# A one-core decoder block: the MLP's first product by seven quadrant products, a second product of its own stage, one DRAM record per retention chunk

## The chip, the core and the metric

The kernel runs on one core of a Trainium2 chip. A core has a matrix engine (TensorE, PE in the profile, its weight loads PEld), three engines for elementwise work (VectorE = DVE, ScalarE = ACT, GpSimd = POOL), and SyncE (SP), whose queue issues nearly all DMAs of this kernel. Each engine takes its instructions in one fixed order and waits for the others through semaphores. The metric is the device time of one execution in microseconds (us). The time of the kernel before is 2742.19 us, the median of 3 runs (2741.0 to 2742.73).

## The reference, cut to what matters

One layer on 1024 tokens of width 1024, float32:

```
h = rms_norm(x, g_mix);  z = h @ w_in                    # 1024 x 13312
rq, rk, rv, rg, dq, dk, dv, cq, gates = split_cols(z)
ret  = swish(rg) * head_norm(retention_chunkwise(rq, rk, rv))   # 4 heads, chunks of 128
y_ret, y_diff, y_cross = ret @ w_ret_o, da @ w_diff_o, ca @ w_cross_o
merged = g0 * y_ret + g1 * y_diff + g2 * y_cross
x = x + merged @ w_out
u = relu(rms_norm(x, g_ffn) @ w_up);  x = x + (u * u) @ w_down    # width 4096
out = rms_norm(x, g_final)
```

`rms_norm(x, g)` multiplies every token by its own factor 1/sqrt(mean(x*x) + eps) and every feature by g.

## The kernel before, in words

**Layout and arithmetic.** Activations are kept feature-major: 128 features in the partitions, 512 tokens (half of the sequence, t = 0 or 1) along a row. Every float32 operand is split into a high part (a CAST on ACT, L141) and a low part (a subtraction on DVE, L142) by `split`, and every product is three matmuls, high by high, high by low, low by high (`mm3`, L154 to L156).

**Stages.** In order of time in the profile: the start and the norm (to 90 us), the combined input projection (to 1128), cross-attention (to 1200), differential attention (to 1437), retention (to 1816), the rest of the retention branch's output projection (to 1930), `w_out` and the second norm (to about 2021), the MLP (to 2732), and the last norm.

**The seven-product scheme** (`left_operands` L207, `quad` L226, `seven` L240) serves the input projection in both kernels. A unit is 256 output columns by all 1024 tokens over all 1024 features. Cut into quadrants it would take eight products of 4 x 3 matmuls of 128x512; Strassen's scheme in Winograd's form takes seven, from four sums of weight quadrants (`add` on DVE in `left_operands`) and four sums of activation quadrants (made once, called T1 to T4), with B11, B21, B22 the plain quadrants. Results are combined through copies s1 to s3 and additions in `emit`. The projection has 52 units.

**Scratch in DRAM.** The projection's results go to DRAM and are read back by the branches. For retention these are several tensors: `zh_d` (q and k, split, 512 tokens of a head), `zt_d` (k and v transposed, split) and `z_d` (the swish gate). For chunk c of head h, `ret_prepare` (L806) computes the masked 128x128 scores (`rsc`) and loads v (two DMAs, L821) and transposed k (L827); `ret_inputs` (L797) loads q and k of a whole head in four DMAs; `ret_product` (L830) makes the chunk's output (`ro`) and the new state (`rst`, `Sf`, `Shl`); `ret_store` (L890), one chunk later, transposes the output (`rot`), loads the gate (`sg`, two DMAs, L898), multiplies on DVE (`spill`) and stores to `rn_d` (two DMAs, L901).

**Fill.** `branch_halves` (L488) is a generator; each step is one product `y` of 24 matmuls of 128x512 of a branch's output projection, multiplied by its gate `g` (loaded, L495) and added to the running sum `m`, which is loaded from and stored to DRAM (`mg_d`, L498, L505). `fill` takes such steps between the chunks of attention and retention; the lists `FILL_D` and `FILL_R` say how many. In differential attention 16 steps of the cross branch run, in retention 16 of the differential branch and about half of the 32 of the retention branch; `drain` takes the rest. `ad_load` (L791) and `ret_features` (L906) read the branches' results back from DRAM, 256 KB a DMA, and split them; they use the `hf` buffers, of which there are two.

**MLP.** `mlp_up` (L1003) makes one 128-wide slice f of u for each token half by 24 matmuls (`fm_gemm`), then relu, square, split; `mlp_down` (L1018) multiplies two slices at a time by `w_down` and adds the 16 results `dn` into `x2` in SBUF on DVE (L1032). The two alternate, so u never leaves SBUF. PSUM has 8 banks: 3 `mm`, 3 `at`, 2 `sc`.

**Order.** Instructions are traced in the program's order, which gives their priority; the framework then fixes each engine's order when the kernel is compiled, and may take a later instruction that is ready by its own reckoning ahead of an earlier one that is not. A pool's memory that another pool used waits tile by tile for its release.

## Time and profile before

| | us |
|---|---|
| median of 3 runs | 2742.19 (2741.0 to 2742.73) |
| the profiled execution's own time | 2745.52 |
| its span, first to last instruction | 2743.7 |
| PE busy in it | 2624.5 (96%) |
| DVE busy | 1550.9 (57%) |
| ACT busy | 979.0 (36%) |

The page has the busy time of each engine, the span in 40 slices, the DMA queues, the chain that ended last, the costliest groups of instructions and the DMA issues. A matmul's time in a row overlaps its neighbours': a 128x512 one shows about 390 ns, and they follow each other faster than that. What one costs is read from how many fit into a stretch in which PE never rests.

### The profile page before, as it was taken

The page shows a single profiled execution, that of the slowest core. Times are in us where ns is not written, and L with a number is a line of the kernel's source. Part 1 is how long each engine was busy: PE and PEld are TensorE (multiplying, and loading weights), DVE is VectorE, ACT ScalarE, POOL GpSimd, SP SyncE. Part 2 cuts the span into 40 slices and gives each one's busy share as a digit, 9 for nine tenths or more (in the row PEclk, how much of TensorE's full clock was granted, in tenths as well). Part 3 has the DMA queues.
Part 4 walks back from the last instruction along what each step waited for, and adds up shares of the span by engine and source line. Part 5 has one row for each costly group of instructions (what it writes and reads, how often), then busy time and mean ns, then how long its engine had stood idle before and what let it go on. Part 6 is the DMA issues. An engine that isn't in the chain of part 4 may idle for free.

```text
span 2743.7 us, 32286 instructions
## 1 busy us (share of the span) xinstructions
PE 2624.5 (96%) x12070; PEld 2139.7 (78%) x12070; DVE 1550.9 (57%) x2745; ACT 979.0 (36%) x1784; POOL 84.9 (3%) x103
## 2 busy tenths in 40 slices
PE   7899999999999999799987898899999999999998
PEld 6688887887888888688875676768788888888887
DVE  6756556665566544377665556544664454544445
ACT  4444444444444444355553223221431212121222
POOL 3000000000000000001110000000000000000001
PEclk9999999999999999999998999989999999999999
DMA  5444447645533332545538878855421111111111
GB/s 204 166 162 170 161 143 222 207 154 149 155 104 111 112 104 92 199 171 194 193 122 292 273 255 257 261 175 166 142 85 46 47 46 54 43 58 47 46 39 62
DMA packets 250221, 390.40 MB, mean 142 GB/s; under 512 B 16720, under 2 KB 150864, under 8 KB 243920
## 3 DMA queue, kind: packets, MB, share of 16 engines
q1 hardware_dynamic: 249920, 388.30, 43.1%
q8 instruction: 95, 1.56, 0.2%
q14 instruction: 62, 0.51, 0.1%
q10 hardware_dynamic: 144, 0.03, 0.0%
HBM read 260.35 MB, written 127.93 MB: 142 GB/s over the span
## 4 chain that ended last, share of the span: by engine, by line
PE 56%; issue 27%; DMA 8%; DVE 6%; ACT 2%; SPq 1%; POOL 1%; POOLq 0%; DVEq 0%; ACTq 0%
PE x L154 12%; PE x L156 12%; PE x L155 12%; PE y L154 3%; PE y L156 3%; PE y L155 3%; DMA g<-z 2%; DMA adr<-da 2%; DMA arr<-rn 1%; PE wo L155 1%; PE wo L156 1%; PE zt L449 1%; PE wo L154 1%; DVE hop L142 1%; DVE g L159 1%
## 5 line engine op out<-in xcount | busy, mean ns | idle before, releaser
L154 PE MATMUL x<-hop,wo 128*128 128x512 f32 x1456 | 572.4, 393 | 6.1 <-ACT wo L141 5.4
L155 PE MATMUL x<-hop,wo 128*128 128x512 f32 x1456 | 574.0, 394 | 0.0
L156 PE MATMUL x<-hop,wo 128*128 128x512 f32 x1456 | 571.5, 393 | 0.0
L154 PEld LDWEIGHTS x<-hop,wo 128*128 128x128 f32 x1456 | 274.1, 188 | 64.6 <-ACT wo L141 5.8
L156 PEld LDWEIGHTS x<-hop,wo 128*128 128x128 f32 x1456 | 274.1, 188 | 58.9 <-DVE wo L142 0.2
L155 PEld LDWEIGHTS x<-hop,wo 128*128 128x128 f32 x1456 | 273.9, 188 | 58.6
L141 ACT CAST whl<-wst 128x1024 fp32r<-128x1024 f32 x112 | 115.9, 1048 | 398.4 <-PE dn L156 257.2
L1032 DVE TENSOR_TENSOR x<-x,dn 128x512 f32<-128x512 f32 (+1 forms) x248 | 164.5, 669 | 128.0 <-PE dn L156 127.6
L155 PE MATMUL dn<-u,whl 128*128 128x512 f32 (+1 forms) x544 | 207.3, 381 | 0.0
L154 PE MATMUL dn<-u,whl 128*128 128x512 f32 (+1 forms) x544 | 206.4, 379 | 0.0
L156 PE MATMUL dn<-u,whl 128*128 128x512 f32 (+1 forms) x544 | 204.5, 376 | 0.0
L155 PE MATMUL u<-h,whl 128*128 128x512 f32 x512 | 200.5, 392 | 0.0
L154 PE MATMUL u<-h,whl 128*128 128x512 f32 x512 | 200.0, 391 | 0.0
L141 ACT CAST wo<-wr 128x512 fp32r<-128x512 f32 x208 | 129.0, 622 | 198.9 <-PE x L156 193.3
L156 PE MATMUL u<-h,whl 128*128 128x512 f32 x512 | 199.4, 389 | 0.0
L159 DVE TENSOR_TENSOR zo<-x,s 128x512 f32<-128x512 f32 x156 | 107.6, 690 | 156.0 <-ACT s L269 106.2
L142 DVE TENSOR_TENSOR wo<-ws,wo 128x512 fp32r<-128x512 f32 x156 | 107.7, 691 | 154.8 <-ACT wo L141 154.8
L142 DVE TENSOR_TENSOR wo<-wr,wo 128x512 fp32r<-128x512 f32 x208 | 142.8, 688 | 69.8 <-ACT wo L141 61.2
L1010 DVE TENSOR_TENSOR ur<-ur 128x512 f32<-128x512 f32 x64 | 44.3, 692 | 194.9 <-ACT ur L1009 194.9
L142 DVE TENSOR_TENSOR whl<-wst,whl 128x1024 fp32r<-128x1024 f32 x112 | 135.4, 1220 | 26.7 <-ACT whl L141 26.6
L1009 ACT ACTIVATE ur<-u 128x512 f32<-128x512 f32 x64 | 38.2, 598 | 233.4 <-PE u L156 233.4
L159 DVE TENSOR_TENSOR g<-y,g 128x512 f32<-128x512 f32 x64 | 44.2, 690 | 133.3 <-PE y L156 80.3
(227 smaller groups left out, 4664.0 us busy)
## 6 DMA issues: line engine op xcount, KB each, us to landing
wr<-in_w_z SPq DMA_DIRECT2D x104, 512.0 KB, 3.8
zh<-zh SPq DMA_DIRECT2D x80, 512.0 KB, 3.5
zt<-zth SPq DMA_DIRECT2D x64, 512.0 KB, 3.8
z<-zo SPq DMA_DIRECT2D x80, 256.0 KB, 2.0
g<-z SPq DMA_DIRECT2D x64, 256.0 KB, 4.6
vhl<-zt SPq DMA_DIRECT2D x64, 256.0 KB, 4.6
wst<-in_w_up SPq DMA_DIRECT2D x32, 512.0 KB, 3.3
wst<-in_w_down SPq DMA_DIRECT2D x32, 512.0 KB, 3.3
```

Of the source, the lines that this page charges most:

```text
L141: nc.scalar.copy(out=hl_hi, in_=src)
L142: eng.tensor_tensor(out=hl_lo, in0=src, in1=hl_hi.bitcast(F32), op=ALU.subtract)
L154: nc.tensor.matmul(out, ah, bh, start=first, stop=False, skip_group_check=again)
L155: nc.tensor.matmul(out, ah, bl, start=False, stop=False, skip_group_check=again)
L156: nc.tensor.matmul(out, al, bh, start=False, stop=last, skip_group_check=again)
L159: nc.vector.tensor_tensor(out=out, in0=a, in1=b, op=op)
L449: nc.tensor.transpose(out=tp[:, i * P : (i + 1) * P], in_=st[:, i * P : (i + 1) * P], identity=ident)
L1009: nc.scalar.activation(out=r, in_=o, func=AF.Relu)
L1010: nc.vector.tensor_tensor(out=r, in0=r, in1=r, op=ALU.mult)
L1032: nc.vector.tensor_tensor(out=x2[d][t][:, cols], in0=x2[d][t][:, cols], in1=o[:, :width], op=ALU.add)
```

## The change

The first product of the MLP is computed by the seven-product scheme, in 16 units, on activations that carry the feature factor `g_ffn` but not the token factor; that factor multiplies the results in `u_emit` before the square (relu commutes with a positive factor). The results go to DRAM (`u_d`), x after the mixer goes there too (`xs_d`), and the second product is a stage of its own that reads both back, with four slices in a product instead of two. In retention, q, k, v, transposed k and the gate of one chunk lie side by side in one DRAM record (`rc_d`, 12 KB a partition), loaded by one DMA; the projection's stores into it become runs of 128 tokens (512 bytes). The running sum of the branches stays in SBUF from the differential branch on (`x2`). Results are read back in pairs (`pair_load`). Four fill steps of the cross branch move from differential attention to the first two retention chunks. PSUM becomes 2 `mm`, 3 `at`, 3 `sc`.

```diff
-FILL_D = [[1, 0] * 4] * 4
-FILL_R = [[1] * 8] * 4
+FILL_D = [[1, 0] * 4] * 2 + [[1, 0, 0, 0] * 2] * 2
+FILL_R = [[2, 2] + [1] * 6] + [[1] * 8] * 3
+C_K, C_Q, C_V, C_KT, C_G, C_N = 0, 512, 1024, 2048, 2560, 3072
...
-        return ps.tile([P, HALF], F32, tag="mm", name=name, bufs=3)
+        return ps.tile([P, HALF], F32, tag="mm", name=name, bufs=2)
...
-        return ps.tile([P, HALF], F32, tag="sc", name=name, bufs=2)
+        return ps.tile([P, HALF], F32, tag="sc", name=name, bufs=3)
...
+        def store_chunks(h, base, width, at, tile):
+            for a in range(2):
+                o = base + a * width + at
+                nc.sync.dma_start(
+                    out=rc_d[h][t][:, :, o : o + P], in_=tile[:, a].rearrange("p (i c) -> p i c", i=4).bitcast(F32)
+                )
...
+                if mode == 1:
+                    nc.sync.dma_start(out=x2[d][t], in_=mg_d[d][t])
                 add(g, o, g, ALU.mult)
+                if mode == 0:
+                    nc.sync.dma_start(out=mg_d[d][t], in_=g)
                 else:
+                    add(x2[d][t], x2[d][t], g)
...
+    def pair_load(src, outs):
+        raw = rawp.tile([P, 4, 2, P], F32, tag="pr", name="pr", bufs=2)
+        nc.sync.dma_start(out=raw, in_=src)
+        for e, o in enumerate(outs):
+            by = o.rearrange("p a (i c) -> p a i c", i=4)
+            split(by[:, 0], by[:, 1], raw[:, :, e])
...
+    def ret_prepare(h, c):
+        rec = rp.tile([P, C_N], F32R, tag="rec", name="rec", bufs=3)
+        nc.sync.dma_start(out=rec.bitcast(F32), in_=rc_d[h][c // 4][:, c % 4])
...
+            if h == 0 and c == 2:
+                drain()
+                ad_load()
+                halves = branch_halves(1, w_do, 0, hl_rhs(ad), 1)
...
+                add(xr, o, xr)
+                nc.sync.dma_start(out=xs_d[d][t], in_=xr)
+                nc.scalar.activation(
+                    out=x3[kp][t][:, a], in_=xr, func=AF.Copy, scale=vec[:, V_FFN + d : V_FFN + d + 1]
+                )
+                sq = zs_tile("acc", "acc") if acc is None else zs_tile("sq", "sq", 1)
+                nc.scalar.activation(out=sq, in_=xr, func=AF.Square)
...
+                    nc.gpsimd.tensor_tensor(out=acc, in0=acc, in1=sq, op=ALU.add)
+            if t == 1:
+                for a in range(2):
+                    operand(h2p, hop2, kp, (B11, B21)[a], x3[kp][0][:, a])
+                operand(h2p, hop2, kp, B22, x3[kp][1][:, 1])
+                t1 = h2p.tile([P, HALF], F32, tag="tt", name="t1", bufs=4)
+                add(t1, x3[kp][1][:, 0], x3[kp][0][:, 0], ALU.subtract)
+                add(x3[kp][0][:, 0], x3[kp][1][:, 1], t1, ALU.subtract)
+                t1s.append(t1)
...
+    def u_emit(u, n, t, a, b):
+        st = zs_tile("sp", "uo", 3)
+        if b is not None:
+            add(st, a, b)
+            a = st
+        nc.vector.scalar_tensor_tensor(out=st, in0=a, scalar=0.0, in1=rows[t], op0=ALU.max, op1=ALU.mult)
+        nc.scalar.activation(out=st, in_=st, func=AF.Square)
+        nc.sync.dma_start(out=u_d[2 * u + n][t], in_=st)
+    for key, t in ((T3, 1), (T4, 0)):
+        for kp in range(4):
+            df = h2p.tile([P, HALF], F32, tag="tt", name="df", bufs=4)
+            nc.gpsimd.tensor_tensor(out=df, in0=x3[kp][t][:, 1], in1=x3[kp][t][:, 0], op=ALU.subtract)
+            operand(h2p, hop2, kp, key, df)
+    seven(list(range(16)), hop2, lambda u: left_operands(wu, w_up[u, 0], w_up[u, 1]), ut, u_emit)
...
+    FC = 4
+    CHUNKS = [range(0, 2), range(2, 4)] + [range(f, f + FC) for f in range(4, 32, FC)]
+    x2 = [[dw.tile([P, HALF], F32, name=f"xm{d}_{t}", tag=f"xm{d}_{t}", bufs=1) for t in range(2)] for d in range(8)]
...
-    mlp_up(range(3))
-    for c in range(nchunk - 2):
-        mlp_up([3] if c == 0 else range((c + 1) * FC, (c + 2) * FC))
+    nxt = down_chunk(0)
+    for d in range(8):
         for t in range(2):
+            nc.sync.dma_start(out=x2[d][t], in_=xs_d[d][t])
+    for c in range(len(CHUNKS)):
+        cur = nxt
+        if c + 1 < len(CHUNKS):
+            nxt = down_chunk(c + 1)
+            for t in range(2):
+                mlp_down(cur, t)
```

## Rows read from the trace of the kernel before

**Rows 1.** The page's busy time of each engine, and its 40 slices of PE
```profile
PE 2624.5 (96%) x12070; PEld 2139.7 (78%) x12070; DVE 1550.9 (57%) x2745; ACT 979.0 (36%) x1784; POOL 84.9 (3%) x103
...
PE   7899999999999999799987898899999999999998
```

**Rows 2.** Busy time by stretch: from:to, us, engines, clock, DMA share, GB/s
```profile
450.00:480.00 30.00, 28.33 (x135) 22.28 (x133) 19.49 (x31) 14.38 (x26) 0.00 (x0) 1.00 0.69 214
...
1127.00:1147.00 20.00, 7.54 (x38) 6.78 (x38) 6.86 (x13) 7.83 (x16) 0.00 (x0) 0.70 0.86 319
...
1200.00:1437.00 237.00, 228.24 (x1316) 191.00 (x1314) 162.55 (x522) 126.77 (x343) 25.11 (x32) 1.00 0.45 155
...
1437.00:1455.00 18.00, 4.62 (x17) 3.99 (x18) 1.17 (x4) 1.75 (x6) 0.39 (x1) 0.56 1.00 371
...
1455.00:1816.00 361.00, 324.69 (x1469) 257.40 (x1468) 217.85 (x470) 101.56 (x165) 19.21 (x32) 0.96 0.80 255
...
1816.00:1930.00 114.00, 108.03 (x425) 81.62 (x423) 44.27 (x60) 22.00 (x31) 0.00 (x0) 0.91 0.51 166
...
2070.00:2670.00 600.00, 600.00 (x2630) 493.43 (x2629) 282.05 (x381) 115.69 (x164) 0.00 (x0) 1.00 0.15 47
```

**Rows 3.** Groups by shape: the MLP's matmuls, and the elementwise work that moves
```profile
L155 PE MATMUL u<-h,whl 128*128 128x512 f32 x512 | 200.5, 392 | 0.0
...
L155 PE MATMUL dn<-u,whl 128*128 128x512 f32 x480 | 188.9, 394 | 0.0
...
L142 DVE TENSOR_TENSOR wo<-wr,wo 128x512 fp32r<-128x512 f32 x208 | 142.8, 688 | 69.8 <-ACT wo L141 61.2 <-DMA wr<-in_w_z 8.7
...
L141 ACT CAST wo<-wr 128x512 fp32r<-128x512 f32 x208 | 129.0, 622 | 198.9 <-PE x L156 193.3 <-DMA wr<-in_w_z 4.3 <-issue 1.3
...
L358 POOL TENSOR_TENSOR xr<-xr 128x512 f32<-128x512 f32 x4 | 6.5, 1634 | 6.2 <-DVE tt L159 6.2
```

**Rows 4.** Timeline of the projection's end and the next stage's first matmul
```profile
1127.96 0.40 PE L156 MATMUL x<-hop,wo 128*128 128x512 f32 x1
...
1132.16 0.85 SPq L541 DMA_DIRECT2D cq<-zh  x2
...
1138.94 0.55 PE L154 MATMUL csc<-mk,cq 128*128 128x256 f32 x1 [10.58 <-DMA cq<-zh]
```

**Rows 5.** Timeline of the start, where POOL and DVE work side by side
```profile
74.92 1.65 POOL L358 TENSOR_TENSOR xr<-xr 128x512 f32<-128x512 f32 x1 [2.43 <-DVE tt L159]
75.37 1.75 DVE L159 TENSOR_TENSOR tt<-xr,tt 128x512 f32<-128x512 f32 x1
```

**Rows 6.** The chain that ended last, at the start of retention
```profile
1436.61 7.54 DMA rk<-zh
...
1444.63 10.99 DMA adr<-da
```

**Rows 7.** Timeline of retention chunks: scores, transposes, the gate's multiplication
```profile
1710.33 0.22 PE L154 MATMUL rsc<-rq,rk 128*128 128x128 f32 x1
...
1710.39 0.27 PE L155 MATMUL rsc<-rq,rk 128*128 128x128 f32 x1
...
1714.61 0.60 PE L893 MATMUL rot<-ident,on 128*128 128x128 f32 x4
...
1812.26 0.60 PE L893 MATMUL rot<-ident,on 128*128 128x128 f32 x4
...
1813.48 0.67 DVE L159 TENSOR_TENSOR spill<-rot,sg 128x512 f32<-128x512 f32 x1
```

**Rows 8.** DMA issues: count, KB each, median us from issue to landing
```profile
zh<-zh SPq DMA_DIRECT2D x80, 512.0 KB, 3.5
zt<-zth SPq DMA_DIRECT2D x64, 512.0 KB, 3.8
...
cq<-zh SPq DMA_DIRECT2D x8, 1024.0 KB, 4.9
...
rk<-zh SPq DMA_DIRECT2D x8, 1024.0 KB, 7.5
```

More of the change, by code (lines that the diff above doesn't have):

```diff
@@ L26 @@
 NH = 4
-NA, NRAW, NLOW = 27, 3, 6
 LAM_INIT = 0.8 - 0.6 * math.exp(0.0)
@@ L110, in hybrid_block @@
     nc.vector.memset(mhalf, -0.5)
-    def pairs(name, n):
-        return [[dram.tile([P, 2, HALF], F32, name=f"{name}{i}_{t}", tag=f"{name}{i}_{t}") for t in range(2)] for i in range(n)]
     def scratch(name, shape):
@@ L486, in fm_gemm, with branch_halves @@
         return out
-    def branch_halves(b, w, w0, rhs, before, out=None):
+    def branch_halves(b, w, w0, rhs, mode):
         for d in range(8):
@@ new lines, in hybrid_block @@
+        rows.append(acc)
+    for kp in range(4):
+        operand(h2p, hop2, kp, T2, x3[kp][0][:, 0])
+    for kp in range(4):
+        operand(h2p, hop2, kp, T1, t1s[kp])
+    for t in range(2):
+        rb = rms_finish(rows[t], HALF)
+        rows[t] = zs_tile("hf", "row")
+        nc.scalar.copy(out=rows[t], in_=rb)
+    wpx.close()
+    ux = ExitStack()
+    wu = ux.enter_context(tc.tile_pool(name="wu", bufs=2, side="right", reuse_waits="tile"))
+    ut = ux.enter_context(tc.tile_pool(name="ut", bufs=2, side="right", reuse_waits="tile"))
@@ new lines, in down_chunk @@
+    def down_chunk(c):
+        ws, us = [], [[], []]
+        for f in CHUNKS[c]:
+            for t in range(2):
+                raw = dw.tile([P, HALF], F32, tag="ur", name="ur", bufs=4)
+                nc.sync.dma_start(out=raw, in_=u_d[f][t])
+                u = dw.tile([P, 2, HALF], F32R, tag="u", name="u", bufs=4 * FC)
+                split(u[:, 0], u[:, 1], raw)
+                us[t].append(u)
+            raw = dw.tile([P, 1024], F32, tag="wr", name="dwr", bufs=2)
+            nc.sync.dma_start(out=raw, in_=w_down[f])
+            w = dw.tile([P, 2, 1024], F32R, tag="w", name="dw", bufs=FC + 3)
+            split(w[:, 0], w[:, 1], raw)
+            ws.append(w)
+        return ws, us
```

293 lines of the change are left out of this document (116 added, 177 removed).

## The prediction

> **What bounds the kernel now.** I read the engines' busy times first, then the slices, then the busy time by stretch, and only then single rows. PE is busy 96% of the span, DVE 57% [rows 1], and PE's slices dip in three places: the start, the 17th slice (where cross-attention begins) and the slices of retention, the 21st to the 26th [rows 1]. By stretch, the MLP has 600 us in which PE never rests: 2630 matmuls, so one costs 600 / 2630 = 0.228 us [rows 2]. There, only fewer matmuls or new holes change the time. Retention and what follows it, 1437 to 1930, is different. Its work by the code: 48 fill products of 24 matmuls, 168 `rst` and 264 `ro` make 1584 of 512 columns, at 0.228 us 361 us; 192 `rsc` and 128 transposes are a few per cent of that. The `rsc` start 0.06 us apart, and four transposes take 0.60 us with the last one's tail, some 0.11 us each [rows 7]: another 25 us. So 386 us of work stand in 493 us, and 107 us are lost. They lie in three places: 18 us at the start, where PE is busy 4.62 us at a clock of 0.56 and the DMA engines are full; 361 us of chunks with a clock of 0.96 and a DMA share of 0.80; and the last 114 us, whose 425 matmuls would need 97 [rows 2]. The chain shows the start waiting 7.54 us for k and then 10.99 us for the differential branch's results [rows 6].
>
> **The change part by part.** The sum is made against the profiled execution, 2745.5 us (span 2743.7), which is 3.3 us above the median of 2742.2.
>
> *First product.* Before: 32 slices by 2 halves by 24 matmuls = 1536, of which the row shows one of three groups of 512 [rows 3]. After: 16 units of 7 x 12 = 1344. 192 fewer at 0.228 us: **-43.8 us**. The second product keeps its count (three groups of 480 wide ones [rows 3], and the halved ones of the end). A unit now needs DVE 4 sums and 7 low parts of the weights, 3 additions and 4 scalings: 18 instructions of about 0.69 us [rows 3] = 12.4 us under 84 x 0.228 = 19.2 us of PE; ACT has 7 casts of 0.62 us and 7 more operations of that size, 8.7 us. Both are covered, as in the projection, whose 52 units have the same form. In the second product DVE adds half as often, but splits u again after its trip through DRAM: per four slices 8 low parts of u (0.69), 4 of w (twice as wide, 1.4 at most) and 16 additions, 22 us under 192 x 0.228 = 43.8 us of PE. Covered too.
>
> *The two new seams in the MLP* are not covered, and no row shows them. Seam one is from `w_out` to the first unit. Two quads (B11, B21: 24 matmuls, 5.5 us) use token half 0 and can run at once. The third needs T2 of the last feature block: its addition, the ACT copy, two subtractions and the split, about 6 x 0.69 = 4.1 us after the last matmul; but T1 and T2 take the place of the `w_out` operands, so their 8 low parts (5.5 us on DVE) all come after that matmul, followed by 8 low parts of T3 and T4, the weight operands of unit 1 (7.6 us) and unit 0's results (5 us). That is some 27 us of DVE in the 19 us that unit 0 gives PE. At best the order hides it (0); at worst 8 us are missing plus what POOL takes. I take **+6 us**, range 0 to 15. Seam two is from the last unit to the first `dn`: result, scaling, square, store, then loads, casts, matmul, all in memory that the units still held. The nearest row is the projection's end, which has the same form: last matmul 1127.96, next stage's load issued 1132.16, its first matmul 1138.94, an idle time of 10.58 us [rows 4]. After it the granted clock was low, 0.70 over the 20 us around it, partly at the lower of its two levels, 1.2 instead of 2.4 GHz [rows 2], which cost some 3 us more. Some of the new loads may be issued before the last store, which would leave 0; at most it is 14. I take **+8 us**, since the memory is reused tile by tile. The MLP: -43.8 + 6 + 8 = -30 us.
>
> *POOL.* 14 sums of squares and 8 differences (T3, T4) go to POOL, 1.63 us each [rows 3]. A row shows what that does to DVE: a subtraction of two SBUF tiles took 1.75 us beside a POOL operation of 1.65, [rows 5] against 0.69 for its like [rows 3]. The sums lie beside `w_out`, where DVE has slack; the 8 differences lie in seam one, and if each holds DVE for 1.75 - 0.69 = 1.06 us, 8.5 us come on top of its 6. That is the upper end of seam one's range. The Trainium skill, "SBUF — State Buffer", section "Who interferes with whom", speaks against this placement: a DVE instruction with two SBUF inputs and a GpSimd instruction that reads SBUF exclude each other, and the second one fully blocks. By that rule every difference costs its full overlap, and the time would come out 9 us later; without it, as summed. The trace agrees with its direction in the 1.75 us; no run shows which of them overlap in the new order.
>
> *Projection stores.* q, k and the gate were stored in runs of 2 KB and go out in runs of 512 bytes, and every split tile by two DMAs. Transposed k and v already use 512-byte runs, and land in 3.8 us against 3.5 [rows 8]. SP has more to issue; the four units of rk, which store both forms, are the tight ones: their stretch has DMA at 0.69 and PE idle 1.7 of 30 us [rows 2]. At worst each of the four loses 2 us more; at best the high half, which leaves before the low half is computed, frees the buffer sooner. **+3 us**, range -3 to 8.
>
> *Retention.* Bytes per chunk are the same, 1.5 MB, but eleven DMA issues of a chunk (v 2, k 1, gate 2, results 2, g, m, sum, half a weight, half a q or k) become about four. The sum in SBUF removes 32 loads and 32 stores of 256 KB of `mg_d`. Four products (4 x 24 x 0.228 = 21.9 us) leave differential attention, whose PE is busy 228.2 of 237 us [rows 2], and come under the start, where PE is idle. I give attention -19 of these 21.9, as its own latencies have less cover. Retention's work becomes 386 + 22 = 408 us. The lost time: at the start one DMA brings all of chunk 0 and four products stand ready: 18 -> 8. At the end pairs of 512 KB halve the number of turns of the two buffers: 17 -> 8. In the chunks 107 - 18 - 17 = 72 us over 31 chunks are lost now, 2.3 us each; fewer issues, less DMA and half the turns at the two reloads should leave 1.5, 48 us. Together 64 instead of 107. **-43 + 22 - 19 = -40 us**. The bounds of the chunk term are far apart. Below: 0.5 us each, 16 us in all, -32 more. Above: the record's three buffers. A record is held from its load until the gate's multiplication one chunk after its product, so the load for chunk n+2 is issued only after the multiplication of chunk n-1, in chunk n. From the scores to the transposes it is 1714.61 - 1710.33 = 4.28 us, from there to the end of the multiplication 1814.15 - 1812.26 = 1.89 us [rows 7], then some 0.6 us to issue. A load of 1 MB lands in 4.9 to 7.5 us [rows 8]; half a MB more at the 371 GB/s of the full DMA [rows 2] adds 1.4: 6.3 to 8.9. Where the next scores stand first on PE, a chunk then can't take less than 6.8 + 6.3 = 13.1 to 15.7 us, against the forecast's (310 + 48) / 32 = 11.2 us (310 us of work: 34 products and the chunks' own). Where PE has the next product ahead of these scores, the trip has 2 to 4 us more room and hides. I take the second, because the compile-time order puts a later ready instruction ahead of one that waits; nothing in the trace of before decides it.
>
> *The rest* (one `mm` bank fewer, one `sc` more, stores of x, the tail): each `mm` result leaves PSUM in 0.69 to 1.3 us while the next product takes 1.4 to 5.5, so two banks do; 0 us, -2 to +3.
>
> Sum: -30 + 3 - 40 = **-67 us**: 2745.5 - 67 = 2678.5 for the profiled execution, and 2742.2 - 67 = 2675 for the median of runs.
>
> **Rivals.** (a) The DMA traffic was all that held retention: chunks lose 0.5 us, and one seam is hidden. -67 - 32 - 8 = -107, 2635 us. For it: the DMA share of 0.80 and a chain that names loads; against: dependencies of state, mask and norm remain. (b) The record's ring binds: every chunk waits for its load, 14.4 us instead of 11.2. 32 x 3.2 = +102, so +35 and 2777 us, slower than before. It decides from 11.2 + 67 / 32 = 13.3 us per chunk, a landing later than 6.5 us with the scores first. For it: 1 MB loads of before landed in 7.5 us [rows 8]; against: that was with four of them queued at once. At about that point it cancels the gain: 2742. (c) The seams eat most of the MLP's gain: 15 and 14 us, and the second stage starved another 10 by its reload of x (4 MB at 371 GB/s is 11 us). +25 on the forecast, 2700 us. For it: the row of the projection's end [rows 4]; against: 5.5 us of work in hand at seam one.
>
> **How the numbers follow.** Forecast 0.48; (a) 0.19; (c) 0.14; (b) slower 0.13, and about its point 0.06 within 0.2% (5.5 us, about what a measurement of this kernel can tell from no change). Faster: 0.48 + 0.19 + 0.14 = 0.81; same 0.06; slower 0.13. The range reaches to (a) with its projection term at its lower end, 2630, and past (c) with the chunks 1 us worse each, 2732; it leaves out (b).
>
> **What would show it.** `x` groups of the first product with 448 matmuls each and 0.228 us apart; an idle time of PE at each seam of 0 to 15 us; in retention a mean over 32 chunks of about 11.2 us and a DMA share under 0.75; the first scores within 10 us of attention's end. The prediction is wrong if the scores wait for `rec` in every chunk (then (b)), if the chunks come near 10.1 us (then (a)), or if a seam shows more than 15 us.

## The result, and the profile after

The changed kernel takes **2705.4 us** (median of four runs, 2703.3 to 2710.3) against 2742.5 us of the kernel before beside it (2741.0 to 2744.5): a ratio of 0.9867, 95% interval 0.985 to 0.9884. That is 37 us faster. The forecast was 67 us faster, 2675 us, with 2630 to 2732 as its range: the direction was right and the time lies in the range, but 30 us of the gain are missing. The profiled execution has a span of 2701.5 us, 42.2 less than the one before; the medians of all runs, 37 us apart, are the safer measure.

Line numbers are 3 higher than in the kernel before (the split's cast is L144, its low part L145; the three matmuls of a product L157 to L159). The page's busy times, its slices of PE and PE's granted clock by slice:

```profile
PE 2577.4 (95%) x11878; PEld 2104.3 (78%) x11878; DVE 1591.9 (59%) x2831; ACT 1057.1 (39%) x1942; POOL 120.4 (4%) x125
...
PE   7899999999999999899998899999979999899998
...
PEclk9899999999999999999998999999989999899999
```

PE has 192 instructions fewer, as counted, and 47 us less of busy time. The dips of attention and retention are shallower than in [rows 1], and there are two new ones, the 30th and the 35th slice: the seams. The stages in us, from start to start of the first or last matmuls named, in the two traces:

| stage | before | after | difference | forecast |
|---|---|---|---|---|
| start to the projection's first `x` | 90.1 | 93.7 | +3.6 | 0 (-2 to +3) |
| projection, to the first `csc` | 1048.8 | 1048.7 | 0 | +3 (-3 to +8) |
| attention, to the last `dot` | 299.2 | 284.6 | -14.6 | -19 |
| retention, to the first `wo` | 491.1 | 467.5 | -23.6 | -21 |
| `w_out` | 91.6 | 88.9 | -2.7 | 0 |
| MLP, last `wo` to last `dn` | 710.8 | 705.6 | -5.2 | -30 |
| the rest | 12.1 | 12.4 | +0.3 | 0 |
| span | 2743.7 | 2701.5 | -42.2 | -67 |

One term failed, the MLP. Its busy times by stretch, with retention's ahead of them (from:to, us, busy us and instructions of PE, PEld, DVE, ACT, POOL, PE's granted clock, DMA share, GB/s):

```profile
1427.00:1443.00 16.00, 9.87 (x32) 7.62 (x33) 6.93 (x16) 3.94 (x8) 0.54 (x1) 0.57 0.91 359
1443.00:1790.00 347.00, 321.04 (x1481) 256.97 (x1480) 215.12 (x458) 98.94 (x162) 17.25 (x30) 0.98 0.72 244
1790.00:1895.00 105.00, 102.28 (x446) 82.23 (x444) 46.52 (x68) 22.96 (x35) 0.83 (x1) 1.00 0.41 130
1895.00:1983.50 88.50, 87.86 (x383) 71.85 (x383) 56.32 (x68) 44.94 (x70) 22.49 (x14) 1.00 0.47 158
1983.50:2008.00 24.50, 9.85 (x28) 5.71 (x27) 20.38 (x31) 9.92 (x18) 15.59 (x11) 0.60 0.23 75
2008.00:2300.00 292.00, 292.00 (x1276) 239.53 (x1275) 178.90 (x278) 125.37 (x215) 0.00 (x0) 1.00 0.30 104
...
2315.60:2330.00 14.40, 6.92 (x16) 4.34 (x15) 6.33 (x8) 4.87 (x7) 0.00 (x0) 0.64 0.93 323
2330.00:2352.00 22.00, 22.00 (x98) 18.12 (x98) 17.15 (x25) 7.73 (x11) 0.00 (x0) 1.00 0.82 290
2352.00:2365.00 13.00, 8.53 (x29) 5.90 (x28) 11.45 (x17) 7.93 (x11) 0.00 (x0) 0.87 0.92 290
```

From 2008 on PE is never idle in the units: 292 us for 1276 matmuls, 0.229 us each, as forecast. The first product as a whole (last `wo` 1983.5 to last `x` 2315.6) takes 332.1 us where 1344 x 0.229 = 307.6 would do: **seam one costs 24.5 us**, not 6. In those 24.5 us PE issues 28 instructions, only six of them for the units, at a granted clock of 0.60 on average, and DVE is busy for 20.4. At seam two 7.8 us pass from the start of the last `x` to that of the first `dn`, 7.45 of them idle, as forecast (8); but in the first 41.6 us after that PE gets through 138 matmuls, which are 31.6 us of work: another 10 us. The lost time of the two seams is 24.5 + 7.8 + 10 = 42 us instead of 14.

Seam one in the timeline (start, us, engine, line, operation, in brackets the idle time before it and what ended it). `hop` is an operand of the units, `df` a difference for T3 or T4. The name `wo` stands for two things: w_out's result (`xr<-wo` adds it to x; "the last `wo`" is its last matmul) and, as `wo<-wr`, a unit's weights.

```profile
1981.45 4.75 DVE L145 TENSOR_TENSOR hop<-t,hop 128x512 fp32r<-128x512 f32 x3 [0.34 <-ACT hop L144]
1982.24 1.75 POOL L992 TENSOR_TENSOR acc<-acc,sq 128x512 f32<-128x512 f32 x1
1983.94 3.38 POOL L1030 TENSOR_TENSOR df<-x 128x512 f32<-128x512 f32 x2
...
1988.40 0.68 DVE L162 TENSOR_TENSOR xr<-wo,xr 128x512 f32<-128x512 f32 x1
...
1992.22 0.80 PE L157 MATMUL x<-hop,wo 128*128 128x512 f32 x1 [7.53 <-ACT wo L144]
...
1996.37 2.48 DVE L145 TENSOR_TENSOR hop<-df,hop 128x512 fp32r<-128x512 f32 x4
...
1996.50 2.08 PE L183 MATMUL rb<-dg,ones 128*128 128x512 f32 x2 [3.48 <-DVE dg L179]
...
1997.19 5.70 POOL L1030 TENSOR_TENSOR df<-x 128x512 f32<-128x512 f32 x3 [2.28 <-DVE hop L145]
...
2004.93 2.05 PE L183 MATMUL rb<-dg,ones 128*128 128x512 f32 x2 [3.37 <-DVE dg L179]
...
2006.51 0.68 DVE L145 TENSOR_TENSOR wo<-wr,wo 128x512 fp32r<-128x512 f32 x1
...
2007.24 0.80 PE L159 MATMUL x<-hop,wo 128*128 128x512 f32 x1 [0.27 <-DVE wo L145]
```

Read it from the end. The third matmul of the very first product (L159) needs the low part of unit 0's weights, and DVE comes to that low part only at 2006.51, after everything that stands ahead of it in its order: the splits of T1 and T2, all eight of T3 and T4, and the token factor. The addition for the last `wo`, on which the last block's x, its square and its operands rest, comes at 1988.40, 4.9 us after PE's last matmul, because five splits stand before it.

### The profile page after: what moved, and what is told of

It is laid out like the page before. It is cut to its first block, busy times and chain, and to the rows that moved or that the text cites. A ratio compares the mean times of both kernels' runs of the same rounds, so it can differ in the third digit from the quotient of the medians.

```text
span 2701.5 us, 32578 instructions
## 1 busy us (share of the span) xinstructions
PE 2577.4 (95%) x11878; PEld 2104.3 (78%) x11878; DVE 1591.9 (59%) x2831; ACT 1057.1 (39%) x1942; POOL 120.4 (4%) x125
## 5 line engine op out<-in xcount | busy, mean ns | idle before, releaser
L157 PE MATMUL x<-hop,wo 128*128 128x512 f32 x1904 | 749.4, 394 | 14.8 <-ACT wo L144 13.2
L158 PE MATMUL x<-hop,wo 128*128 128x512 f32 x1904 | 749.1, 393 | 0.0
L159 PE MATMUL x<-hop,wo 128*128 128x512 f32 x1904 | 747.4, 393 | 0.3 <-DVE wo L145 0.3
L157 PEld LDWEIGHTS x<-hop,wo 128*128 128x128 f32 x1904 | 358.7, 188 | 91.3 <-ACT wo L144 13.6
L159 PEld LDWEIGHTS x<-hop,wo 128*128 128x128 f32 x1904 | 358.4, 188 | 79.7 <-DVE wo L145 2.1
L158 PEld LDWEIGHTS x<-hop,wo 128*128 128x128 f32 x1904 | 358.5, 188 | 77.4
L144 ACT CAST wo<-wr 128x512 fp32r<-128x512 f32 x272 | 168.3, 621 | 239.2 <-PE x L159 231.4
L145 DVE TENSOR_TENSOR wo<-ws,wo 128x512 fp32r<-128x512 f32 x204 | 140.5, 690 | 198.1 <-ACT wo L144 198.1
L145 DVE TENSOR_TENSOR wo<-wr,wo 128x512 fp32r<-128x512 f32 x272 | 186.5, 687 | 91.4 <-ACT wo L144 79.0
L157 PE MATMUL dn<-u,dw 128*128 128x512 f32 (+1 forms) x544 | 207.5, 382 | 12.2 <-ACT dw L144 7.4
L158 PE MATMUL dn<-u,dw 128*128 128x512 f32 (+1 forms) x544 | 207.0, 381 | 0.0
L159 PE MATMUL dn<-u,dw 128*128 128x512 f32 (+1 forms) x544 | 206.1, 379 | 0.0
L162 DVE TENSOR_TENSOR xm<-xm,dn 128x512 f32<-128x512 f32 (+1 forms) x152 | 99.0, 656 | 145.0 <-PE dn L159 144.6
L144 ACT CAST wo<-ws 128x512 fp32r<-128x512 f32 x204 | 126.3, 621 | 83.3 <-PE x L159 75.8
L157 PEld LDWEIGHTS dn<-u,dw 128*128 128x128 f32 x544 | 103.3, 190 | 33.7 <-ACT dw L144 8.5
L159 PEld LDWEIGHTS dn<-u,dw 128*128 128x128 f32 x544 | 103.3, 190 | 20.0 <-DVE dw L145 0.8
L158 PEld LDWEIGHTS dn<-u,dw 128*128 128x128 f32 x544 | 103.5, 190 | 19.2 <-issue 0.2
L162 DVE TENSOR_TENSOR g<-y,g 128x512 f32<-128x512 f32 x64 | 44.1, 689 | 112.9 <-PE y L159 94.3
L157 PE MATMUL y<-ar,whl 128*128 128x512 f32 x256 | 102.1, 399 | 3.5 <-ACT ar L144 3.5
L144 ACT CAST whl<-wst 128x1024 fp32r<-128x1024 f32 x48 | 50.4, 1051 | 134.3 <-PE y L159 93.3
L158 PE MATMUL y<-ar,whl 128*128 128x512 f32 x256 | 101.4, 396 | 0.9 <-DVE ar L145 0.9
```

What stands on the lines that cost most here:

```text
L144: nc.scalar.copy(out=hl_hi, in_=src)
L145: eng.tensor_tensor(out=hl_lo, in0=src, in1=hl_hi.bitcast(F32), op=ALU.subtract)
L157: nc.tensor.matmul(out, ah, bh, start=first, stop=False, skip_group_check=again)
L158: nc.tensor.matmul(out, ah, bl, start=False, stop=False, skip_group_check=again)
L159: nc.tensor.matmul(out, al, bh, start=False, stop=last, skip_group_check=again)
L162: nc.vector.tensor_tensor(out=out, in0=a, in1=b, op=op)
```

## The experiments

Each kernel was timed beside the kernel before, on the chip it ran on. The table has medians, and the lengths of the stages in the profiled execution (us); "second" is from the first `dn` to the last. Stages vary between profiles of the same code: the first product by 1.2 us (332.0 to 333.2 where no edit touches it), attention by 3.5, retention by 9 (465.5 to 474.9). So one profile shows effects above some 1 us in the first product, and in retention only those above some 10 us.

| kernel | median | ratio, 95% interval | start | attention | retention | `w_out` | first product | second |
|---|---|---|---|---|---|---|---|---|
| after | 2705.4 | 0.985 to 0.9884 | 93.7 | 284.6 | 467.5 | 88.9 | 332.1 | 365.7 |
| e1_df_vector | 2710.7 | 0.986 to 0.9909 | 92.5 | 287.4 | 467.9 | 88.9 | 336.3 | 364.8 |
| e3_x_halves | 2703.7 | 0.9842 to 0.9877 | 94.3 | 288.1 | 474.9 | 88.9 | 333.2 | 362.3 |
| e4_gate_apart | 2686.4 | 0.9788 to 0.982 | 94.9 | 287.3 | 445.8 | 88.9 | 332.8 | 364.3 |
| e6_slots | 2705.4 | 0.9853 to 0.9882 | 94.4 | 285.3 | 469.0 | 88.9 | 333.0 | 365.1 |
| e5_banks | 2702.3 | 0.984 to 0.9876 | 89.4 | 289.7 | 465.0 | 88.9 | 332.0 | 365.1 |
| e7_row | 2716.3 | 0.988 to 0.9921 | 94.1 | 287.2 | 471.4 | 95.5 | 331.4 | 364.4 |
| e8_slots_row | 2704.3 | 0.9841 to 0.9871 | 94.8 | 287.5 | 469.0 | 94.5 | 321.6 | 365.7 |
| e12_no_df | 2700.8 | 0.982 to 0.9877 | 92.4 | 287.5 | 465.5 | 88.9 | 322.4 | 364.8 |
| e13_no_row | 2707.9 | 0.9851 to 0.9885 | 93.1 | 286.8 | 473.5 | 88.9 | 329.4 | 365.0 |
| e9_all | 2680.6 | 0.9759 to 0.981 | 94.6 | 287.9 | 443.6 | 94.5 | 320.3 | 362.1 |
| e10_all_later | 2676.5 | 0.9744 to 0.9787 | 92.3 | 287.6 | 447.7 | 92.1 | 322.3 | 363.0 |
| e11_all_banks | 2683.4 | 0.9762 to 0.9798 | 91.0 | 288.8 | 453.4 | 92.1 | 322.7 | 362.3 |

The first product's length is seam one plus 1344 matmuls, and these don't go at one pace in all profiles. From the 200th to the 1200th, one takes 228.9 ns from start to start in the kernel after and in ten others, and 233.3 ns in e1_df_vector and e6_slots: 6.0 us more over 1344, without idle time and at a granted clock of 1.00. The same 100 us of the units in the kernel after, in e1_df_vector and in e6_slots:

```profile
2100.00:2200.00 100.00, 100.00 (x439) 82.05 (x438) 60.34 (x94) 43.00 (x74) 0.00 (x0) 1.00 0.33 113
...
2100.00:2200.00 100.00, 100.00 (x430) 81.00 (x429) 59.77 (x92) 42.23 (x72) 0.00 (x0) 1.00 0.31 106
...
2100.00:2200.00 100.00, 100.00 (x430) 81.23 (x429) 59.40 (x92) 42.26 (x73) 0.00 (x0) 1.00 0.31 107
```

No run shows why. So the seam itself is the first product less 1344 matmuls at the profile's own pace: 24.5 us in the kernel after (24.4 to 25.5 where no edit touches it), 22.7 in e1_df_vector, 19.4 in e6_slots, 23.8 in e7_row, 14.0 in e8_slots_row, 14.8 in e12_no_df, 21.7 in e13_no_row and 12.7 in e9_all.

**Seam one: the differences on DVE.**

```diff
-            nc.gpsimd.tensor_tensor(out=df, in0=x3[kp][t][:, 1], in1=x3[kp][t][:, 0], op=ALU.subtract)
+            nc.vector.tensor_tensor(out=df, in0=x3[kp][t][:, 1], in1=x3[kp][t][:, 0], op=ALU.subtract)
```

> One change to the kernel after: the eight differences of seam one (`df`, for T3 and T4) are computed by DVE instead of POOL. Theory A (POOL beside DVE lengthens the seam): the splits beside them fall from 1.58 us to about 0.7, which gives some 7 us back, and the differences cost DVE 8 x 0.69 = 5.5 us; the first product's stage (332 us from the last `wo` to its end, where its 1344 matmuls alone need 308) shrinks by 2 to 4 us. Theory B (DVE has too much work in the seam, whoever blocks it): the stage grows by 3 to 6 us. Theory C (neither: memory that comes free late, loads behind a store): within 1 us.

The stage grew by 4.2 us, which is theory B's number but not its cause: the slower matmuls make 6.0 us, and the seam itself is 1.8 us shorter, somewhat less than theory A's 2 to 4 and little more than its spread. The splits that took 1.58 us each beside POOL now take 0.67 to 0.69, but for one beside one of POOL's sums (1.66), so POOL did hold DVE; but the differences are work that DVE has to do as well. Of the 24.5 us behind the last `wo` DVE is busy for 21.7:

```profile
1985.50:2010.00 24.50, 12.65 (x34) 7.85 (x33) 21.66 (x42) 11.80 (x23) 4.40 (x3) 0.60 0.22 75
```

**Seam one: operands that don't wait for the last matmul.**

```diff
-    AM = [(B11, B21), (T1, T2)]
+    AM = [(B11, B21), (T3, T4)]
...
-            x3[kp][t] = h2p.tile([P, 2, HALF], F32, tag=f"op{kp}_{(T4, T3)[t]}", name="x3")
+            x3[kp][t] = h2p.tile([P, 2, HALF], F32, tag=f"op{kp}_{(T1, T2)[t]}", name="x3")
...
+                add(d3, x3[kp][1][:, 1], x3[kp][1][:, 0], ALU.subtract)
+                add(d4, x3[kp][0][:, 1], t2, ALU.subtract)
+                operand(h2p, hop2, kp, T2, t2)
+                operand(h2p, hop2, kp, T1, t1)
```

> Two changes to the kernel after, both in seam one: the operands of `w_out`'s token half 1 lie where T3 and T4 will be (needed fifth and seventh) instead of T1 and T2 (third and fourth), so that T1 and T2 of a block are split as soon as its x is there; and the eight differences are computed by DVE, into tiles that are free by then, as part of `w_out`'s work. Theory A (the seam is made of splits that have to wait for the last `w_out` matmul, because their memory holds its operands): the first product's stage falls from 332 us by 10 to 16 us. Theory B (POOL beside DVE made it): no better than with the differences on DVE alone. Theory C (`w_out`'s stage has no room on DVE for the work moved into it): its 89 us grow by what the seam loses.

No gain in the stage: 333.0 us. Its slower matmuls hide that the seam fell from 24.5 to 19.4 us, about half of what theory A said. The work did leave the seam (DVE busy 18.5 of 24.5 us, `w_out` as long as before), but PE's first matmul of unit 0 came even later, 14.1 us after the last `wo`. PE stood at the token factor, and ACT's first cast of the unit's weights stood behind the copy of that factor:

```profile
1986.90:2011.40 24.50, 13.24 (x47) 9.45 (x46) 18.52 (x37) 10.83 (x20) 3.31 (x3) 0.65 0.38 124
...
1997.62 2.08 PE L183 MATMUL rb<-dg,ones 128*128 128x512 f32 x2 [9.54 <-DVE dg L179]
1999.73 0.58 ACT L1013 COPY row<-rb 128x512 f32<-128x512 f32 x1 [3.60 <-PE rb L183]
2000.22 1.14 ACT L144 CAST wo<-wr 128x512 fp32r<-128x512 f32 x2
```

**Seam one: the token factor elsewhere.** Half 0's is finished after `w_out`'s first half, half 1's is spread only when unit 0 has a result for it.

```diff
-        rows.append(acc)
+        rows.append(rms_finish(acc, HALF, True))
+        if t == 0:
+            row_factor(0)
...
     def u_emit(u, n, t, a, b):
+        if (u, n, t) == (0, 1, 1):
+            row_factor(1)
```

> One change to the kernel after: of the token factor's work that stood between `w_out` and the first unit, half 0 is done right after `w_out`'s first half, and the spreading of half 1 (`dg`, `rb`, `row`) waits until unit 0 has its first result of half 1. Theory A (seam one is the row factor: PE, ACT and DVE keep their written order, and stand before it while the first unit could run): PE no longer stops at `rb` between the first matmuls of `x`, and the first product's stage falls from 332 us by 6 to 12 us. Theory B (the seam is set by the first operands and weights themselves, the row factor only fills a wait): within 2 us.

Theory B: 331.4 us, and 0.7 less in the seam. And it cost 6.6 us in `w_out`, where PE now stops for POOL's last addition to half 0's sum; the factor's matmuls follow, and the granted clock is 0.98 over the stage, which had 1.00:

```profile
1952.52 1.05 PE L170 MATMUL ssq<-ones,acc 128*128 128x1 f32 x8 [1.98 <-POOL acc L1001]
...
1902.00:1997.50 95.50, 92.88 (x395) 73.81 (x393) 57.62 (x73) 45.65 (x71) 23.34 (x15) 0.98 0.43 146
```

**Both together** (the two edits above):

> The edits of e6_slots and e7_row together. In e6_slots the operands were ready early, but the first `x` matmul came only 14 us after the last `wo`: ACT had the copy of the row factor ahead of its first cast of `w_up`, and that copy waited for PE's `rb`, which waited for DVE's `dg`. Theory A (two causes in a row, each of which hides the other): the stage falls from 332 to about 316 to 322 us, more than e6_slots (333) and e7_row together give. Theory B (the edits add up and neither hides the other): as e7_row, within 2 us. Theory C (the first load of `w_up`, queued on SP behind the last stores of x, then decides): the stage stops at about 320 with the first `x` some 8 us after the last `wo`.

Now the first product takes 321.6 us and the seam 14.0, 10.5 less than in the kernel after, where the edits alone took 5.1 and 0.7 off the seam: theory A, by some 4.7 us. Two causes stood side by side, and each hid a part of the other. (The stage's lengths alone, +0.9 and -0.7, would say that each hid all of it.) In the 24.5 us behind the last `wo` PE issues 63 instructions instead of 28, 53 of them for the units instead of six:

```profile
1994.50:2019.00 24.50, 17.44 (x63) 13.59 (x62) 23.47 (x39) 13.78 (x25) 2.66 (x2) 0.79 0.51 168
```

Theory C's signs fit too: the first `x` comes 8.9 us after the last `wo`. But in e9_all below, where the first `w_up` load is issued 0.1 us after the last `wo` instead of 3.2, the first `x` still comes 8.4 us after it and the stage is only 1.3 us shorter. The load isn't what is left of the seam.

`w_out` gave 5.6 us back, for the reason shown by e7_row, and the median, 2704.3 us, can't be told from that of the kernel after.

**How much of seam one is the work itself?** Two kernels leave work out. The first doesn't compute T3 and T4 and uses other operands in their place; the second leaves out the token factor's finish and scales by other values.

```diff
-            nc.gpsimd.tensor_tensor(out=df, in0=x3[kp][t][:, 1], in1=x3[kp][t][:, 0], op=ALU.subtract)
-            operand(h2p, hop2, kp, key, df)
+        hop2[kp][T3], hop2[kp][T4] = hop2[kp][T1], hop2[kp][T2]
```

> The kernel after without the eight differences of seam one and their splits: T3 and T4 are not computed, the units read T1's and T2's operands in their place (the same count of matmuls, other values). It takes 8 operations of 1.3 to 1.7 us from POOL, 8 casts from ACT and 8 low parts from DVE. Theory A (the seam is the amount of elementwise work in it: DVE is busy 20.4 of the 24.5 us behind the last `wo`): the first product's stage falls from 332 to 320 to 325 us. Theory B (the seam is a chain: last result, its scaled copy, first weights, the token factor in the engines' written order): it stays within 3 us.

```diff
-        rb = rms_finish(rows[t], HALF)
         rows[t] = zs_tile("hf", "row")
-        nc.scalar.copy(out=rows[t], in_=rb)
+        nc.scalar.activation(out=rows[t], in_=x3[0][t][:, 1], func=AF.Copy, scale=1.0)
```

> The kernel after without the token factor's finish: the sums of squares are still added up, but `ssq`, `dg` and `rb` are left out, and the factor's tile is a copy of a block of x, so the first product's results are scaled by other values; everything else stays. Theory A (amount of work): DVE loses 8 short scalings, 2.3 us with what goes with them; the first product's stage falls from 332 by 2 to 3 us. Theory B (the token factor's chain stands in PE's, ACT's and DVE's order ahead of the first unit): PE's two stops at `rb` (3.48 and 3.37 us) go with their half clock, and the stage falls by 6 to 12 us.

Both came out as theory A said: the stage fell by 9.7 us without the eight differences and their splits (322.4), and by 2.7 us without the token factor (329.4). Without the factor PE has no stop at `rb`, and still only 18 instructions in 24.5 us, because DVE, busy for all of them, comes no earlier to the weights. That isn't amount of work alone: eight of DVE's 26 operations there took 1.74 to 1.76 us beside POOL, where one alone takes 0.68. These are 8.5 us; in the kernel after the same holding makes 5.7 us of the 24.5. With the factor gone POOL held DVE longer, so the 2.7 us needn't be all that the factor costs. The 24.5 us behind the last `wo` in e12_no_df, then in e13_no_row:

```profile
1983.84:2008.34 24.50, 19.20 (x68) 14.23 (x67) 21.84 (x42) 12.60 (x23) 3.66 (x3) 0.72 0.46 144
```

```profile
1991.40:2015.90 24.50, 6.87 (x18) 4.24 (x17) 24.50 (x26) 11.57 (x21) 13.73 (x9) 0.58 0.25 82
```

**Retention: the gate out of the record.**

```diff
-        rec = rp.tile([P, C_N], F32R, tag="rec", name="rec", bufs=3)
-        nc.sync.dma_start(out=rec.bitcast(F32), in_=rc_d[h][c // 4][:, c % 4])
+        rec = rp.tile([P, C_G], F32R, tag="rec", name="rec", bufs=3)
+        nc.sync.dma_start(out=rec.bitcast(F32), in_=rc_d[h][c // 4][:, c % 4, :C_G])
+        sg = rp.tile([P, HALF], F32, tag="sg", name="sg", bufs=3)
+        nc.sync.dma_start(out=sg, in_=rc_d[h][c // 4][:, c % 4, C_G:])
```

> One change to the kernel after: the gate leaves the retention record (10 KB a partition instead of 12, three buffers as before) and comes by a DMA of its own into three buffers of 2 KB, so that a record is free after its product, not after the gate's multiplication a chunk later. Theory A (the record's three buffers hold the chunks, the forecast's rival b in part): PE's waits for the record, 23.5 us in 19 times, fall to under 10 us, the mean chunk from 11.5 to about 11.0 us, the time by 10 to 18 us. Theory B (the load's own time, 7 to 8 us at the DMA rate there, holds them, or other waits take over): within 4 us, and the waits stay or move to the gate or the products.

Theory A, and a little more than it said: 2686.4 us, 19 less than after, with retention 22 us shorter. All matmuls that read the record waited for its load 37 times in the kernel after, for 50.9 us (PE and its weight loads counted apart; PE alone 19 times, 23.5 us), and 4 times for 11.4 us with the gate apart (PE alone 2 times, 5.2 us). After, then e4_gate_apart: the idle times that the record's load ended, and the same stretch of 317 us:

```profile
  DMA rec<-rc: 50.9, 37
...
1443.00:1760.00 317.00, 292.50 (x1346) 234.09 (x1345) 196.98 (x418) 90.00 (x148) 15.63 (x27) 0.97 0.74 251
```

```profile
  DMA rec<-rc: 11.4, 4
...
1443.00:1760.00 317.00, 303.01 (x1429) 248.41 (x1428) 203.59 (x443) 95.02 (x160) 17.72 (x28) 0.98 0.80 268
```

The mean chunk (31 steps from the first to the last `on`, the normalised output of a chunk) falls from 11.51 to 10.85 us, and the DMA share rises from 0.74 to 0.80: DMA throughput wasn't the limit, the buffers were. The smaller record also lands sooner, in 7.2 us instead of 8.1 (medians), but that isn't the reason. In the kernel after 26 of the 29 loads from the fourth on were issued 0.6 to 1.3 us after the gate's multiplication of three chunks before, and in 23 of 32 chunks the scores began within 0.2 us of the landing. With the gate apart 28 of 29 loads were issued before that multiplication, and the record lay ready 8.7 us (median) before its scores.

**Seam two: half of the reload of x behind the next chunk's loads.**

```diff
     for d in range(8):
-        for t in range(2):
-            nc.sync.dma_start(out=x2[d][t], in_=xs_d[d][t])
+        nc.sync.dma_start(out=x2[d][0], in_=xs_d[d][0])
...
             nxt = down_chunk(c + 1)
+            if c == 0:
+                for d in range(8):
+                    nc.sync.dma_start(out=x2[d][1], in_=xs_d[d][1])
```

> One change to the kernel after: of the 16 reloads of x at seam two, the eight of token half 1 are issued after the loads of the second product's chunk 1, not before them. Theory A (the reloads stand in SP's queue ahead of chunk 1 and starve it): the idle time of 4.46 us before chunk 1 and the stretch at half clock after it go, -4 to -8 us; seam two itself (7.84 us from the last `x` to the first `dn`) stays. Theory B (chunk 1 waits for its own buffers or for DMA throughput): the idle time stays, within 2 us, or the additions of half 1 wait for x and PE idles a few us more.

The second product became 3.4 us shorter (362.3 us), just short of theory A's range, and the time (2703.7) can't be told from that of after. The four kernels with this edit have 362.1 to 363.0 us there, the others 364.3 to 365.7. The idle time within chunk 1's products (4.07 us; 4.46 from start to start of the matmuls) turned into three of 1.0 to 1.5, 3.6 in all, and the low clock behind it went (1.00 instead of 0.87), but the waits that are left name neither SP's queue nor a load. What ends the stop is in both kernels an addition on DVE, which frees a PSUM bank. After, then e3_x_halves:

```profile
2349.92 1.28 DVE L145 TENSOR_TENSOR u<-ur,u 128x512 fp32r<-128x512 f32 x2
2351.12 1.22 DVE L145 TENSOR_TENSOR dw<-dwr,dw 128x1024 fp32r<-128x1024 f32 x1
...
2356.32 1.28 DVE L162 TENSOR_TENSOR xm<-xm,dn 128x512 f32<-128x512 f32 x2
2357.05 0.73 PE L157 MATMUL dn<-u,dw 128*128 128x512 f32 x1 [4.07 <-DVE xm L162]
```

```profile
2371.70 0.50 PE L157 MATMUL dn<-u,dw 128*128 128x512 f32 x1 [1.45 <-DVE xm L162]
...
2364.70:2377.70 13.00, 9.37 (x39) 6.76 (x38) 12.01 (x18) 6.26 (x9) 0.00 (x0) 1.00 0.88 290
```

In the kernel after, eight splits for the chunk to come stand between two additions, from 2349.92 to 2356.32; in the other DVE is busy 12.0 of 13 us around the three. So theory A is right that the order of the loads matters, and wrong on what PE waits for.

**The banks of PSUM.**

```diff
-        return ps.tile([P, HALF], F32, tag="mm", name=name, bufs=2)
+        return ps.tile([P, HALF], F32, tag="mm", name=name, bufs=3)
...
-        return ps.tile([P, HALF], F32, tag="sc", name=name, bufs=3)
+        return ps.tile([P, HALF], F32, tag="sc", name=name, bufs=2)
```

> One change to the kernel after: the PSUM banks as they were before, three for `mm` and two for `sc`. Theory A (the third `sc` bank buys nothing, the lost `mm` bank costs the start): the first projection product comes 3 to 4 us earlier (93.7 back to about 90), the stages from cross-attention to the end of retention keep their lengths within 2 us, and the time falls by 3 to 4 us. Theory B (the third `sc` bank carries part of what attention and retention gained): these stages grow by 4 to 15 us and the time is no shorter.

The start is 4.3 us shorter, and retention no longer (465.0, within its spread); attention is 289.7, 1.6 above the largest of the kernels with two `mm` and three `sc` banks. Its time, 2702.3 us, is 3 less than after with overlapping intervals. That the lost `mm` bank costs the start is shown (89.4 us here and 91.0 in e11_all_banks, 92.3 to 94.9 in all kernels with two); what the third `sc` bank gives isn't settled by this run.

**The edits together.** The first adds those of e3, e4, e6 and e7, and two stores on another queue:

```diff
-                nc.sync.dma_start(out=xs_d[d][t], in_=xr)
+                (nc.scalar if t == 1 and kp == 3 else nc.sync).dma_start(out=xs_d[d][t], in_=xr)
```

> The edits of e3_x_halves, e4_gate_apart, e6_slots and e7_row together, and the last two stores of x issued on ACT's queue, so that they don't stand ahead of the first `w_up` loads on SP's. If the places are independent: 2705 - 19 (gate) - 3 (reload of x) - 10 to 16 (seam one) = 2667 to 2673 us. If what one place gives back is taken by the next: 2680 us or more, and the stage that grew shows where.

2680.6 us: retention (443.6), the first product (320.3) and the second (362.1) keep their gains, and `w_out` has e7_row's loss (94.5): the expectation's second case, with `w_out` as the stage that grew. The profiled execution alone (2675.8) is near the sum less that loss.

The next two put half 0's token factor into the middle of `w_out`'s second half and half 1's wholly into unit 0; the second has three `mm` and two `sc` banks as well.

```diff
             if t == 1:
+                if kp == 1:
+                    row_factor(0)
```

> As e9_all, with the token factor placed anew: half 0's in the middle of `w_out`'s second half (after its second pair of blocks) instead of right behind the first half, where PE stopped 2.4 us for the sum and then ran at half clock (`w_out` 94.5 us instead of 88.9); half 1's wholly in unit 0, its sums too, so that PE doesn't stop at `ssq` before the first `x`. Theory A (the stops at `ssq` are what is left of both): `w_out` back to 89 us and the first product's stage from 320 to 312 to 317, 2665 to 2672 us. Theory B (first operands and first weights take as long): `w_out` back to 89, the first product's stage stays at 319 to 321, about 2675 us.

> As e10_all_later, with three `mm` and two `sc` banks as before the change. If the third `sc` bank does nothing even where the records come early enough: 3 to 5 us less than e10_all_later, all of it before the first `x` of the projection (94 back to 90 us). If it then carries the scores ahead: retention's stage grows by 3 us or more and the two times agree.

e10_all_later has the lowest median, **2676.5 us**, ratio 0.9765 (0.9744 to 0.9787): faster than both the kernel before and the kernel after; its interval overlaps e9_all's. Theory B of its two is the nearer one: the first product stays at 322.3, and `w_out` comes back only to 92.1. In the compiled order half 1's `ssq` and `rb` still stand ahead of all of unit 0 (PE idles 4.6 us before the one and 4.5 before the other), and PE's first `x` came 12.3 us after the last `wo`; where the call stands in the program hadn't moved them. e11_all_banks is 7 us slower than e10_all_later, not 3 to 5 faster: the start gained 1.3 us and retention grew by 5.6. That fits a third `sc` bank that carries scores ahead once the records come early, but the two intervals overlap (0.9744 to 0.9787, 0.9762 to 0.9798) and retention varies by that much: it stays open.

## Why the prediction was right or wrong

**First product, 192 matmuls fewer: right.** 0.229 us each without idle time from 2008 to 2300; the units cover their elementwise work, as [rows 3] let expect.

**Seam one: the term that failed.** By the forecast's own sign, a seam of more than 15 us, it is wrong here. It listed the work, some 27 us of DVE, and mis-sized its cover. It set that work beside the 19 us of unit 0 on PE and left 8 us to be missing at worst, 15 with POOL. But a unit can't begin without the low part of its own first weights, and in DVE's order these came after nearly all of the operands' splits. So the 5.5 us of work in hand, and unit 0 with it, began after DVE's work, not beside it. What measures it: 24.5 us; 9.7 of them go with the eight differences and splits (e12), 2.7 with the token factor (e13), and 10.5 when the operands' work moves ahead and the token factor out of the way (e8). No kernel brought the seam under 12.7 us, and what that rest is made of no run took apart. The forecast also took the token factor for free, since it is applied to the results: its chain `ssq`, `dg`, `rb` still stood in the written order of PE, ACT and DVE ahead of the unit, and it kept e6_slots to 5.1 of the 10.5 us. (One reading was off as well: three of T1's four low parts began before the last `wo` matmul, not after it.)

**POOL: right in its mechanism.** Beside POOL's 1.75 us and 3.38 for two, three DVE splits took 4.75 us, 1.58 each, where the like of them take 0.69 [rows 3]: DVE finished one split for each POOL operation. This is the exclusion that the Trainium skill, "SBUF — State Buffer", section "Who interferes with whom", states for a DVE instruction with two SBUF inputs and a GpSimd instruction that reads SBUF; the trace agrees, with 1.58 against 0.69 us. It goes the other way as well: from 1996.37 four splits followed each other in 2.48 us, and the first of POOL's three differences, which began among them, took 2.79 us. The forecast's price of 8.5 us for this holding was too high: six operations of DVE were held in the 24.5 us, for 5.7 us in all (8.5 in e13_no_row). And the remedy is nearly an even trade: the differences cost DVE 8 x 0.69 = 5.5 us, and the seam of e1 is 1.8 us shorter.

**Seam two: right in its 8 us, wrong in "covered".** 7.45 us of idle time, under the 10.58 that [rows 4] showed for the projection's end. The 10 us behind it were in no term of the forecast; some 3 of them are the clock (last section). It summed DVE's work for a chunk of four slices, 22 us under 43.8 of PE. The first two chunks have two slices each: they have the same 16 additions (0.63 to 0.69 us, 10 to 11 us) under 96 x 0.229 = 22 us of PE, and the splits of the first four-slice chunk fall beside the second of them, 8 x 0.64 + 4 x 1.22 = 10 us. That is 21 us of DVE in 22, with the order of the two left to the compiled program; PE waited for additions, which free PSUM banks.

**The MLP as a whole** is rival (c), with a chance of 0.14: its 15 + 14 + 10 = 39 us came out as 24.5 + 7.8 + 10 = 42, and its 2700 us as 2705. That the sums agree is luck: seam one was 24.5 us instead of 15 and seam two 7.8 instead of 14. Its third term was named for the reload of x; what e3 gave back is 3.4 us, and DVE's order and the clock are the rest as far as the waits show.

**Retention and attention: right in the sum, by two errors that cancel.** Together -38 us against -40; the other profiles of the same code have -27 to -37, so the kernel after's own profile is the best of them and the forecast rather too high. By place, with 408 us of work: the start lost some 9 us (16 less 32 x 0.229; forecast 8), the end 3 (105 less 446 x 0.229; forecast 8), which leaves 48 of the 60 lost for the chunks, as forecast. But the forecast held that the record's ring hides because PE has a product ahead of the scores. It didn't hide: e4 took 22 us out of the stage and 0.66 out of the mean chunk of 11.51. Rival (b) was right on the mechanism, with the scores right behind the landing in 23 of 32 chunks, and wrong on the size, 14.4 us a chunk, since PE often did have other matmuls first; and without the ring a chunk takes 10.85 us, less than the forecast's 11.2: the rest of the change gave the chunks more than was reckoned. Which part of it did, fewer issues or less traffic, no run took apart.

**Projection stores: +3 forecast, 0 measured**; the smaller runs are hidden. **The start: 0 forecast, +3.6 measured**, just outside its -2 to +3: the eight `mv` products, of 16 matmuls each, take turns in the `mm` banks while ACT is busy with splits, and the forecast's argument, at most 1.3 us for a result to leave PSUM against at least 1.4 of the next product, was made for PE alone and left out ACT's queue. e5 gives back 4.3. **`w_out`: 0 forecast, -2.7 measured**; no run took that apart.

## What to carry to other kernels

Cost a new seam between two stages by the order on the engine that prepares the operands, not by its total beside PE's: ask what is the last thing the first matmul needs, and count everything that stands ahead of it there. Look for it at every place where the steady state begins, such as a small first chunk, which has the same additions as a large one.

When a removal gives less than it should, try it with the next suspect removed too: here two edits took 5.1 and 0.7 us off a seam, and together 10.5. And before a stage's length is taken for a seam's, compare the pace of its steady part: 4.4 ns more for each of 1344 matmuls made a gain of 5 us look like nothing, and another look like a loss.

A buffer that is held to the end of its last small use (here 2 KB of gate in a record of 12 KB) sets when the next load starts. Splitting it off bought 19 us for one more DMA a chunk.

## What the runs showed of the hardware

The stops of the seams cost more than their idle time: the granted clock was 0.60 over the 24.5 us of seam one and 0.64 over the 14.4 us from the last `x` on, so partly at the lower of its two levels, 1.2 instead of 2.4 GHz. At seam two this can be told apart: after 7.45 us of idle time the 14 `dn` matmuls from 2323.4 to 2330.0 took 6.6 us instead of 3.2, so 3 of the seam's 18 us are the clock. In e3 three idle times of 1.0 to 1.5 us left it at 1.00.

```profile
2323.44 0.80 PE L157 MATMUL dn<-u,dw 128*128 128x512 f32 x1 [7.45 <-ACT dw L144]
...
2323.40:2330.00 6.60, 6.52 (x14) 4.34 (x15) 3.65 (x4) 2.08 (x3) 0.00 (x0) 0.51 1.01 375
```

At a granted clock of 1.00 and without idle time, matmuls of one shape (128x512) followed each other at different paces: 226.7 ns in the second product of all thirteen kernels of the table, 228.9 in the first product of eleven of them and 233.3 in that of two. Why stays open.

Beside POOL, DVE's short scalings by one number a row (`dg`, one tensor as input) were held as well, not only operations with two SBUF inputs. In the kernel after two of them took 1.25 us each beside a difference and a sum of 1.26 us, and four took 0.22 each when POOL was idle; POOL's differences took 1.26 to 2.79.

```profile
1991.20 1.26 POOL L1030 TENSOR_TENSOR df<-x 128x512 f32<-128x512 f32 x1
1991.26 2.50 DVE L179 TENSOR_SCALAR dg<-ident,rr 128x128 f32<-128x128 f32 x2 [0.32 <-POOL rr L176]
...
2003.91 0.87 DVE L179 TENSOR_SCALAR dg<-ident,rr 128x128 f32<-128x128 f32 x4 [2.15 <-POOL rr L176]
```
